# Norm outputs from factors in PSUM without GpSimd, and two output tiles side by side behind each head of a two-block network

## The chip, the cores and the metric

The kernel runs on one NeuronCore of a Trainium2 chip. The metric is the device time of one execution in microseconds (us); less is better. The core has TensorE (matrix products into PSUM), the vector engine (DVE), ScalarE (ACT), GpSimd (POOL), and SyncE (SP), which here only issues transfers.

## What is computed

Two transformer-like blocks, one after the other, on 512 tokens of width 1024. The first has a layer with attention and a long convolution, and a layer that pools over windows of tokens; each is followed by an MLP with squared ReLU. The second has two hybrid layers (a linear recurrence beside an attention with latents, then a gated feed-forward). All of them have the same form, of which this is the core:

```
y = x * rsqrt(mean(x * x) + eps) * g
a = y * (1 + scale) + shift
x = x + gate * (squared_relu(a @ w1) @ w2)
x = x + gate * ((silu(a @ w_gate) * (a @ w_up)) @ w_ffn_out)
proj = a @ w_in
pooled = mean over a window of tokens of a, minus a
```

## The kernel before

Tokens lie along the free dimension: x is eight tiles of 128 channels by 512 tokens. Every fp32 value enters a product as a pair: a high part rounded to 12 bits and a low part, the rest; three products (high with high, low with high, high with low; `mm3`, lines 458 to 460) make one of full accuracy. One output tile of 128 columns is 8 x 3 products of 128x512.

Weights come as portions of 512 KB through six buffers, in an order that `plan` writes down. A portion is loaded by SyncE (line 233), its high part is made by ScalarE (line 255), its low part by a subtraction (line 273). The engine of the subtraction is fixed by a table for some weights (GpSimd for the input weights `xl`, the gates and most of the attention's), and for all others, the MLPs' among them, it is `self.l_eng`. A buffer is loaded anew when the portion in it is done with. `prefetch(n)` emits this work for up to n portions ahead; `consume` takes the next portion and calls `prefetch(self.look)`. Between the weights stand portions of the modulation's matrices (`ada`), summed by GpSimd (lines 371 and 383). In the heads' weights the product with the shift is summed besides (`_shift_step`, line 309, on the vector engine).

All instructions are emitted in the order of the program text; each engine runs its own in that order and waits for the others by semaphores.

A *head* stands before each MLP, each hybrid layer and each gated feed-forward, six in all. `head` starts the first four output tiles of the next product from x times the gains, which needs no norm: 96 products in line 619. Meanwhile the sums of squares (line 574), the inverse roots (`rsqrt`, lines 548 to 556) and their broadcast into a PSUM tile (line 563) are made. ScalarE copies that tile to SBUF (line 636). Then `norm_mod` makes the norm's output for all tiles to come, for each of the eight blocks: a product with the factors (vector engine, line 658), the high part (ScalarE, line 663), the same in full fp32 (GpSimd, line 664), the low part (vector engine, line 682). After each second block a portion of weights is prepared, with GpSimd as `l_eng`. Behind that the head's four tiles are evacuated (line 643 and the caller's `evac`). The next output tiles follow through `gemm`, one after the other; `gemm` has a form `outer=n` that computes n tiles side by side, block by block of the contraction. There are six PSUM buffers for output tiles (`ps`) and two further ones (`pss`, for sums and broadcasts).

In the hybrid layers `conv(0)` to `conv(7)` are the first tiles behind the head, each with three vector operations from PSUM (line 1925); between them the sums of squares of the latents (line 574, from line 542) and their inverse roots and broadcast lie. In the pooling layer (`layer1`) products with the pool's weights come first, two halves (line 1786 evacuates them), then products with window tables, again two halves (line 1812 evacuates them into x, line 603 makes the next head's inputs).

Of the kernel before, what the change touches and what calls it, by code (L numbers as in the profile page):

```python
# [14 lines left out]
AF = mybir.ActivationFunctionType  # L15
# [39 lines left out]
class Weights:  # L55
    """h and l views of one part, by chunk of the contraction"""
# [9 lines left out]
# which engine takes which small operation, and the order of the steps that run beside each other  # L66
# [69 lines left out]
class Prog:  # L136
# [59 lines left out]
    def piece(self, label, src, parts):  # L196
        """src: dram view, rows x blocks x columns; parts: (kind, which blocks and columns of the view, extra), each loaded alone"""
        for kind, (k, n), extra in parts:
            p = dict(label=label, src=src[:, k, n], raw=None)
            self.pieces.append(p)  # L200
            self.parts.append((p, (kind, extra)))

    def wpiece(self, label, w, k0, kc, n0, nc_, by_k=False, shift=None):
        """shift: (layer, which) of the shift whose product with the weights is wanted besides"""
# [112 lines left out]
    def prefetch(self, n_ahead):  # L317
        """splits emitted up to n_ahead weight parts beyond the one consumed last"""
# [47 lines left out]
    def scaled(self, mode, out, x, sc):  # L366
        """out = x * sc, by the vector engine, by GpSimd or by the scalar engine"""
# [7 lines left out]
    def add_scaled(self, mode, out, x, sc):  # L375
        """out += x * sc, by the vector engine, by GpSimd or by the scalar engine and GpSimd"""
# [28 lines left out]
    def ada_tick(self, want=None):  # L405
        """the rest of sums that came ready a while ago, or of those wanted"""
# [14 lines left out]
    def flush_into(self, out, src):  # L421
        """A column of ada_r holds 32 entries, each as the sums over the four quarters of the partitions: add these up
        and put each entry on its partition."""
# [4 lines left out]
    def flush(self, layer):  # L428
        """the modulation vectors that are ready"""
# [32 lines left out]
    def gemm(self, label, x, n_tiles, evac, outer=0, looks=None):  # L462
        """x: list of (h, l) tiles, one for each 128 of the contraction; evac(m, psum)"""
# [38 lines left out]
    def steps(self, gen):  # L502
        """one step of the generator with each tick"""
# [91 lines left out]
    def head_x(self, k):  # L595
        """x times the norm's gains, ahead of the norm"""
# [8 lines left out]
    def head(self, chain, gs, sh, evac):  # L605
        """The first four tiles of a product with a norm's output start from x times the gains; the factor of each token
        and the product with the shift come on behind. chain() gives the factors. Returns the norm's output."""
# [25 lines left out]
        group(range(2, 3))  # L633
        bp = self.bcast(y, 4, self.ps_s, "pss")
        bc = self.get()
        self.S.copy(bc[:], bp[:])
        group(range(3, 8))
        l_eng, self.l_eng = self.l_eng, self.G
        A = self.norm_mod(self.x, bc, gs, sh, each=lambda k: self.prefetch(k // 2 + 1) if k % 2 else None)
        self.l_eng = l_eng  # L640
# [10 lines left out]
    def norm_mod(self, xs, bc, gs, sh, n=T, free=False, each=None):  # L651
        """h/l pairs of x * rstd * gs + sh"""
        out = []
        pend = None
        for k, x in enumerate(xs):
# [6 lines left out]
            else:  # L662
                self.S.activation(r(hl[0])[:, 0:n], t[:, 0:n], AF.Identity, scale=gs[:, k:k + 1], bias=sh[:, k:k + 1])
                self.G.tensor_scalar(y[:, 0:n], t[:, 0:n], gs[:, k:k + 1], sh[:, k:k + 1], op0=ALU.mult, op1=ALU.add)  # L664
# [20 lines left out]
    def gain(self, name, layer, i, g=None, width=8):  # L685
        """g * (1 + scale) as columns"""
# [9 lines left out]
    def sin_red(self, x, out, P, tmp, quarter=False):  # L696
        """out = sin(x), or cos(x); x is kept. In steps"""
# [84 lines left out]
    # parts split ahead by the last products before a norm: the head's parts are through before the last ones  # L782
# [73 lines left out]
    def hyena_filter(self, hd, w3):  # L856
        """Spectrum of the filter, in steps. With t and f both even or odd the transform falls into four of half the size:
# [893 lines left out]
    def layer1(self):  # L1751
# [40 lines left out]
        for half in range(2):  # L1792
# [23 lines left out]
            if half == 0:  # L1816
                self.prefetch(4)
# [583 lines left out]
```

## Time and profile before

| | us |
|---|---|
| median of three runs | 2698.91 (2698.41 to 2698.95) |
| span of the profiled execution | 2697.1 |
| TensorE busy | 2487.8 |
| vector engine busy | 1863.4 |
| GpSimd busy | 1567.3 |
| ScalarE busy | 1106.0 |

The span runs from the first to the last instruction of the one execution that was profiled; the time of a run has 1.8 us more than it by the median, which lie before and behind the instructions. Times within the profile are counted from the span's start. In the span, the first layer takes about 470 us, its MLP goes to about 860, the pooling layer to 895, the second MLP to 1254, the hybrid layers to 1972 and to the end. A row of the timeline gives start and duration in us, engine, line, operation, output and inputs, and in brackets the idle time of the engine before it and what ended that. Neighbours of one line are merged, with their count. DVE is the vector engine, ACT is ScalarE, POOL is GpSimd, PE is TensorE, SPq the queue of SyncE.

### The profile page before, as it was taken

How to read it: one execution, taken by the hardware profiler on the slowest of the kernel's cores; microseconds unless marked ns; L12 is line 12 of the kernel's file. 1: busy time of each engine (PE TensorE's matmuls, PEld its weight loads, DVE VectorE, ACT ScalarE, POOL GpSimd, SP SyncE). 2: the span in 40 equal slices, each digit the busy share in tenths (PEclk: the TensorE clock that was granted, in tenths of full speed). 3: DMA queues.
4: the chain of work that ended last, by engine and by line, in shares of the span. 5: the costliest groups of instructions: out<-in, count | busy, mean ns of one | idle time of the engine just before them, and what ended most of it. 6: DMA issues, size and time to landing. Idle time of an engine off the chain costs nothing.

```text
span 2697.1 us, 32008 instructions
## 1 busy us (share of the span) xinstructions
PE 2487.8 (92%) x11472; PEld 2068.4 (77%) x11472; DVE 1863.4 (69%) x2612; ACT 1106.0 (41%) x2057; POOL 1567.3 (58%) x1250
## 2 busy tenths in 40 slices
PE   7787778999989899999879999999999799999998
PEld 6665667787868688888668887888877688788887
DVE  6899988776666787766888667455477876733334
ACT  3446553433223433334466543222245654423231
POOL 6687756699981689963675348778146744400001
PEclk8788989999989899999889999999999899999999
DMA  7233332366673167662312235666422123233331
GB/s 244 83 118 102 109 94 86 95 191 199 200 218 97 51 177 210 213 177 72 96 57 67 87 92 164 182 192 201 117 75 81 49 81 117 71 102 94 95 91 50
DMA packets 433368, 330.30 MB, mean 122 GB/s; under 512 B 11799, under 2 KB 365207, under 8 KB 433208
## 3 DMA queue, kind: packets, MB, share of 16 engines
q1 hardware_dynamic: 429976, 322.22, 39.8%
q0 software_dynamic: 3232, 6.03, 0.7%
q8 instruction: 90, 1.47, 0.2%
q14 instruction: 70, 0.57, 0.1%
HBM read 319.82 MB, written 8.39 MB: 122 GB/s over the span
## 4 chain that ended last, share of the span: by engine, by line
PE 52%; DVE 8%; POOL 3%; ACT 2%; issue 2%; POOLq 0%; DVEq 0%; ACTq 0%
PE ps L458 16%; PE ps L460 16%; PE ps L459 16%; PE ps L477 2%; PE ps L619 1%; POOL slot L273 1%; DVE slot L1973 1%; POOL slot L664 1%; DVE slot L1925 1%; DVE slot L2038 1%; DVE slot L1961 1%; DVE slot L527 1%; PE ps L2029 0%; DVE slot L682 0%; PE pss L574 0%
## 5 line engine op out<-in xcount | busy, mean ns | idle before, releaser
L458 PE MATMUL ps<-slot 128*128 128x512 f32 (+2 forms) x3120 | 1209.2, 388 | 56.0 <-DVE slot L527 16.8
L460 PE MATMUL ps<-slot 128*128 128x512 f32 (+2 forms) x3120 | 1202.8, 386 | 45.8 <-DVE slot L682 24.7
L459 PE MATMUL ps<-slot 128*128 128x512 f32 (+2 forms) x3120 | 1200.8, 385 | 16.6 <-DVE slot L273 13.5
L458 PEld LDWEIGHTS ps<-slot 128*128 128x128 f32 x3120 | 603.4, 193 | 174.1 <-DVE slot L527 19.6
L460 PEld LDWEIGHTS ps<-slot 128*128 128x128 f32 x3120 | 602.4, 193 | 169.0 <-DVE slot L682 32.7
L459 PEld LDWEIGHTS ps<-slot 128*128 128x128 f32 x3120 | 602.9, 193 | 128.9 <-DVE slot L273 15.2
L255 ACT CAST slot<-raw 128x512 fp32r<-128x512 f32 (+1 forms) x764 | 425.8, 612 | 339.6 <-DMA raw<-in_mlp_w_dram 220.2
L383 POOL TENSOR_TENSOR slot<-slot 128x512 f32<-128x512 f32 x336 | 489.9, 1458 | 57.9 <-ACT slot L373 30.5
L273 DVE TENSOR_TENSOR slot<-raw,slot 128x512 fp32r<-128x512 f32 (+1 forms) x554 | 486.9, 922 | 36.7 <-ACT slot L255 32.0
L542 POOL TENSOR_TENSOR slot<-slot 128x512 f32<-128x512 f32 (+1 forms) x64 | 88.0, 1380 | 555.7 <-ACT slot L536 550.1
L273 POOL TENSOR_TENSOR slot<-raw,slot 128x512 fp32r<-128x512 f32 (+1 forms) x210 | 307.7, 1490 | 141.0 <-ACT slot L255 100.1
L371 POOL TENSOR_SCALAR slot<-raw,cols 128x512 f32<-128x512 f32 x192 | 206.1, 1076 | 58.0 <-DMA raw<-in_w_ada_dram 39.7
L371 POOL TENSOR_SCALAR slot<-raw,s_lat 128x512 f32<-128x512 f32 x144 | 154.9, 1079 | 6.4 <-DMA raw<-in_ada_w_dram 6.3
L619 PE MATMUL ps<-slot 128*128 128x512 f32 x576 | 145.5, 412 | 7.4 <-DVE slot L1812 7.4
L2187 DVE TENSOR_TENSOR slot<-slot,ps 128x512 f32<-128x512 f32 x40 | 27.5, 687 | 175.5 <-PE ps L460 175.5
L536 ACT ACTIVATE slot<-slot 128x512 f32<-128x512 f32 (+1 forms) x98 | 55.3, 575 | 214.4 <-DVE slot L1708 61.4
L619 PEld LDWEIGHTS ps<-slot 128*128 128x128 f32 x576 | 114.0, 200 | 32.5 <-DVE slot L1812 8.3
L526 ACT CAST slot<-slot 128x512 fp32r<-128x512 f32 x80 | 47.1, 619 | 190.0 <-DVE slot L2187 155.8
L664 POOL TENSOR_SCALAR slot<-slot,g,mod 128x512 f32<-128x512 f32 x48 | 57.2, 1198 | 85.8 <-DVE slot L658 85.8
L527 DVE TENSOR_TENSOR slot<-slot 128x512 fp32r<-128x512 f32 x75 | 81.7, 1110 | 35.7 <-ACT slot L526 35.7
L2212 DVE SCALAR_TENSOR_TENSOR slot<-ps,mod,slot 128x512 f32<-128x512 f32 x40 | 30.0, 749 | 102.2 <-PE ps L460 102.2
L416 DVE STREAM_TRANSPOSE slot<-slot 128x512 f32<-128x512 f32 x44 | 31.1, 706 | 94.7 <-POOL slot L383 94.6
(322 smaller groups left out, 2796.7 us busy)
## 6 DMA issues: line engine op xcount, KB each, us to landing
raw<-in_mlp_w_dram SPq DMA_DIRECT2D x128, 512.0 KB, 4.8
raw<-in_w_ada_dram SPq DMA_DIRECT2D x96, 512.0 KB, 4.4
raw<-in_ada_w_dram SPq DMA_DIRECT2D x88, 512.0 KB, 5.0
raw<-in_w_ffn_in_dram SPq DMA_DIRECT2D x88, 512.0 KB, 4.2
raw<-in_w_in_dram SPq DMA_DIRECT2D x56, 512.0 KB, 3.8
raw<-in_w_ffn_out_dram SPq DMA_DIRECT2D x32, 512.0 KB, 5.3
raw<-in_mix_w_dram SPq DMA_DIRECT2D x20, 512.0 KB, 3.9
raw<-in_w_out_dram SPq DMA_DIRECT2D x16, 512.0 KB, 4.1
```

Source lines behind the costliest of these rows:

```text
L255: self.S.copy(r(v), src[:, k:k + kk, :])
L273: eng.tensor_tensor(r(lv), src, v, op=ALU.subtract)
L371: self.G.tensor_scalar(out, x, sc, 0.0, op0=ALU.mult, op1=ALU.add)
L383: self.G.tensor_tensor(out, out, v, op=ALU.add)
L458: self.PE.matmul(out, lhsT=wh, rhs=xh, start=start, stop=False)
L459: self.PE.matmul(out, lhsT=wl, rhs=xh, start=False, stop=False)
L460: self.PE.matmul(out, lhsT=wh, rhs=xl, start=False, stop=stop)
L527: (eng or self.V).tensor_tensor(r(l)[:, 0:n], src, h[:, 0:n], op=ALU.subtract)
L536: self.S.activation(sq[:, 0:n], x, AF.Square, scale=scale)
L542: (eng or self.G).tensor_tensor(st["acc"][:, 0:n], st["acc"][:, 0:n], sq[:, 0:n], op=ALU.add)
L619: PE.matmul(ps[:], lhsT=w[i][:, m * 128:(m + 1) * 128], rhs=r(x[j])[:], start=(k == 0 and n == 0), stop=(k == 7 and n == 2))
L664: self.G.tensor_scalar(y[:, 0:n], t[:, 0:n], gs[:, k:k + 1], sh[:, k:k + 1], op0=ALU.mult, op1=ALU.add)
```

## The change

In the head, the norm's products read the factors where the broadcast left them, in PSUM; the copy to SBUF stays for the evacuations and is made behind the first block. The full fp32 form of each block (line 664) is made by ScalarE. Low parts of weights beside the norm go to the engine that `l_eng` has outside (the vector engine). The first portion is prepared ahead of the broadcast, the others behind the third, fifth and seventh block. Behind the heads, the first two tiles are computed side by side: in the MLPs, in the hybrid layers (`conv2`), and in the feed-forward. In the pooling layer, portions are prepared at other places, and from its second part on by the vector engine. The rest of the diff takes comments out; it is left out here.

```
 head:
         group(range(2, 3))
+        self.prefetch(1)
         bp = self.bcast(y, 4, self.ps_s, "pss")
+        group(range(3, 8))
         bc = self.get()
-        self.S.copy(bc[:], bp[:])
-        group(range(3, 8))
-        l_eng, self.l_eng = self.l_eng, self.G
-        A = self.norm_mod(self.x, bc, gs, sh, each=lambda k: self.prefetch(k // 2 + 1) if k % 2 else None)
-        self.l_eng = l_eng
+
+        def beside(k):
+            if k == 0:
+                self.S.copy(bc[:], bp[:])
+            elif k % 2 == 0:
+                self.prefetch(k // 2 + 1)
+
+        A = self.norm_mod(self.x, bp, gs, sh, each=beside)
 norm_mod:
-                self.G.tensor_scalar(y[:, 0:n], t[:, 0:n], gs[:, k:k + 1], sh[:, k:k + 1], op0=ALU.mult, op1=ALU.add)
+                self.S.activation(y[:, 0:n], t[:, 0:n], AF.Identity, scale=gs[:, k:k + 1], bias=sh[:, k:k + 1])
 mlp:
-        self.gemm("w1", A, 4, lambda m, ps: evac(h0, ps))
+        self.gemm("w1", A, 4, lambda m, ps: evac(h0, ps), outer=2)
 layer1, end of the first loop and second loop:
-            self.prefetch(half + 1)
+            self.prefetch(half + 2)
+        self.l_eng = V
 ...
                 self.head_x(m)
+                if m == 2:
+                    self.prefetch(4)
             self.put(Z, self.pb[2 * half:2 * half + 2])
-            if half == 0:
-                self.prefetch(4)
-        self.l_eng = V
 hybrid:
-        def conv(j):
-            ps = gemm1("xl")
+        def conv2(*js):
+            pss = []
+            self.tick()
+            self.ada_tick()
+            self.gemm("xl", A, 2, lambda m, ps: pss.append(ps), outer=2)
+            conv(js[0], pss[0])
+            self.tick()
+            conv(js[1], pss[1])
+
+        def conv(j, ps=None):
+            ps = ps or gemm1("xl")
 ...
-        conv(0)
-        conv(1)
+        conv2(0, 1)
 up:
-                self.gemm("fg", A, 2, lambda m, ps: evac_g(ps))
+                self.gemm("fg", A, 2, lambda m, ps: evac_g(ps), outer=2 if c == 0 and i == 1 else 0)
```

## Rows read from the trace of the kernel before

**Rows 1.** The page: busy time of TensorE and GpSimd, share, instructions.
```profile
PE 2487.8 (92%) x11472; PEld 2068.4 (77%) x11472; DVE 1863.4 (69%) x2612; ACT 1106.0 (41%) x2057; POOL 1567.3 (58%) x1250
```
**Rows 2.** Waits over the span: who for whom, us in total, times, longest.
```profile
PE ps L460 <- DVE slot L682: 24.7, 18, 2.2
```
**Rows 3.** Timeline of the head and norm at 1615 us.
```profile
1611.41 0.60 PE L563 MATMUL pss<-ident,ny 128*128 128x128 f32 x4
1611.77 13.88 PE L619 MATMUL ps<-slot 128*128 128x512 f32 x60
1612.10 0.59 ACT L636 COPY slot<-pss 128x512 f32<-128x512 f32 x1 [8.34 <-PE pss L563]
1612.72 0.69 DVE L658 TENSOR_TENSOR slot<-slot 128x512 f32<-128x512 f32 x1 [2.69 <-ACT slot L636]
...
1615.04 1.28 DVE L658 TENSOR_TENSOR slot<-slot 128x512 f32<-128x512 f32 x2
1615.76 0.81 ACT L663 ACTIVATE slot<-slot,mod,g 128x512 fp32r<-128x512 f32 x1 [1.43 <-DVE slot L658]
...
1616.48 1.13 ACT L255 CAST slot<-raw 128x512 fp32r<-128x512 f32 x2
1616.94 3.00 POOL L273 TENSOR_TENSOR slot<-raw,slot 128x512 fp32r<-128x512 f32 x2
1617.02 1.78 DVE L682 TENSOR_TENSOR slot<-slot 128x512 fp32r<-128x512 f32 x1 [0.69 <-POOL slot L664]
...
1625.48 0.39 PE L458 MATMUL ps<-slot 128*128 128x512 f32 x1
...
1633.74 0.50 PE L460 MATMUL ps<-slot 128*128 128x512 f32 x1 [2.15 <-DVE slot L682]
...
1634.20 1.75 DVE L682 TENSOR_TENSOR slot<-slot 128x512 fp32r<-128x512 f32 x1 [0.52 <-POOL slot L664]
...
1636.00 0.79 PE L460 MATMUL ps<-slot 128*128 128x512 f32 x1 [1.30 <-DVE slot L682]
```
**Rows 4.** Window of TensorE: length, busy (instructions), granted clock, DMA share, GB/s.
```profile
1636.60:1641.60 5.00, 5.00 (x13) 0.50 0.35 105
```
**Rows 5.** Windows of all engines: length, busy of PE, PEld, DVE, ACT, POOL, clock, DMA.
```profile
530.00:797.00 267.00, 253.46 (x1096) 208.21 (x1095) 183.55 (x192) 81.76 (x145) 257.44 (x210) 0.97 0.64 197
...
1645.00:1972.00 327.00, 327.00 (x1448) 270.91 (x1447) 182.48 (x232) 97.23 (x179) 210.75 (x179) 1.00 0.61 177
```
**Rows 6.** Timeline of GpSimd and of SyncE's queue behind the head at 490.
```profile
526.54 1.21 POOL L371 TENSOR_SCALAR slot<-raw,s_lat 128x512 f32<-128x512 f32 x1 [6.34 <-DMA raw<-in_ada_w_dram]
...
522.62 3.34 SPq L233 DMA_DIRECT2D raw<-in_ada_w_dram  x2
```
**Rows 7.** Timeline of the vector engine: a small norm's product, factors in PSUM.
```profile
1330.68 0.68 DVE L658 TENSOR_TENSOR slot<-slot,ps 128x512 f32<-128x512 f32 x1
```
**Rows 8.** Timeline behind the heads of the hybrid layers, vector engine and TensorE.
```profile
2008.16 2.47 DVE L643 TENSOR_TENSOR slot<-ps,slot 128x512 f32<-128x512 f32 x4
...
2015.92 0.69 DVE L542 TENSOR_TENSOR slot<-slot 128x512 f32<-128x512 f32 x1 [0.36 <-ACT slot L536]
2016.76 3.01 PE L574 MATMUL pss<-ones,slot 128*128 128x1 f32 x16 [2.50 <-DVE slot L542]
2017.11 4.54 DVE L1925 SCALAR_TENSOR_TENSOR slot<-ps,cols,slot 128x511 f32<-128x511 f32 x6 [0.49 <-ACT slot L1923]
...
2022.88 1.19 DVE L554 TENSOR_TENSOR na<-yi 128x4 f32<-128x4 f32 x1
...
1316.70 0.65 PE L563 MATMUL ps<-ident,ny 128*128 128x128 f32 x4 [3.75 <-DVE ny L556]
```
**Rows 9.** Timeline of the pooling layer, vector engine and TensorE.
```profile
882.12 6.78 DVE L309 SCALAR_TENSOR_TENSOR slot<-raw,mod,slot 128x512 f32<-128x512 f32 x4
...
889.61 0.80 PE L619 MATMUL ps<-slot 128*128 128x512 f32 x1 [6.53 <-DVE slot L1812]
```

## The prediction

> **What bounds the kernel now.** I read the page's busy shares first: TensorE is busy for 92% of the span, GpSimd for 58% [rows 1]. So time can be had only where TensorE waits or runs at the lower clock. The list of waits names such a place: it waited 24.7 us, 18 times, for the vector engine's subtraction in line 682, the low part of a norm's output [rows 2]. Cut by window, these are three waits in each of the six heads (about 490, 910, 1275, 1615, 1990 and 2330 us), 24.7 / 6 = 4.1 us a head.
>
> The timeline of one head shows why. The factors' broadcast ends at 1612.0, ScalarE copies it, and the first product starts at 1612.7 [rows 3]. TensorE's 60 head products take 13.88 us, so one takes 13.88 / 60 = 0.23 us, and at 1625.5 it starts the first tile that needs the norm's output. It needs one of the eight blocks every 3 x 0.23 = 0.7 us; the norm's last subtraction ends only at 1634.20 + 1.75 = 1635.95, which is 23.2 us after its start. So TensorE waits, the last times 2.15 and 1.30 us [rows 3]. A vector subtraction takes 0.6 us from start to start where it is undisturbed (two in 1.28 us), but 1.78 us beside a GpSimd subtraction that runs from 1616.94 [rows 3]: the two hold each other up, and both are in this norm's chain.
>
> The waits cost more than themselves. From 1636.6 to 1641.6, behind these waits, the granted clock was 0.50, the 1.2 GHz level [rows 4]. Its 12 products there take 0.43 us instead of 0.23: 12 x 0.2 = 2.4 us, with the two at the edges 2.9 us. The heads at 490, 910 and 2330 have the same pattern.
>
> **What a head is worth depends on what follows it.** From 1645 to 1972 TensorE is busy without a gap, 327.00 of 327 us [rows 5], and likewise from 940 to 1254 and from 2360 to 2660: what the heads at 910, 1615 and 2330 save stays saved. From 530 to 797 it is GpSimd that is full, 257.44 of 267 us, while TensorE has 253.46 [rows 5]: there the end is set by when GpSimd's work begins. Behind the two heads of the hybrid layers (1275, 1990) a chain on the vector engine goes on.
>
> **The change, head by head.** *No GpSimd in the norm.* The added parts are, for each of the eight blocks, one more ScalarE activation in place of the GpSimd operation, and for each of four weight portions two subtractions on the vector engine (in the hybrid heads most stay on GpSimd: the input weights have that engine fixed). The products read the factors in PSUM. The trace has the form: line 658 with one operand in PSUM takes 0.68 us [rows 7], against 0.69 from SBUF [rows 3], so I cost this at nothing and count the copy off the front: the first product starts at 1612.1. The Trainium skill (Perfetto Trace Analysis, Optimizing Scalar/DVE Operations) gives the vector engine about 125 ns of access overhead on PSUM and 60 on SBUF; by it each norm would be 8 x 0.065 = 0.5 us longer, and the sum below 1.5 us smaller, as three heads count it. The two rows above do not show it.
>
> *The new length.* ScalarE's activations start 0.72 us apart (1615.76 to 1616.48), a pair of casts takes 1.13 us [rows 3]. The first block goes through alone: product 0.69, two activations 1.54, subtraction, with hand-overs 3.1 us, and the vector engine's next product stands behind that subtraction. The copy of the factors for the evacuations now lies on ScalarE in that time (0.59 us, [rows 3]). The next product waits for it at most, if the two may not read one bank together, and it is through before the subtraction is. Then three rounds of two blocks and a portion: ScalarE 4 x 0.72 + 1.13 = 4.0 us, the vector engine 6 x 0.6 = 3.6 us, so 4.2 us with a hand-over; last block 3.1. Together 3.0 + 3 x 4.2 + 3.1 = 18.7 us, so the end is at 1630.8, against 1635.95: 5.1 us earlier. The bound on the other side: GpSimd, now free, can begin its modulation sums inside the norm and hold up the vector engine. One portion of these is loaded by then, three operations in the price of up to 1.1 us each (1.78 - 0.69): 1634.
>
> *Two tiles side by side.* TensorE now takes 6 products for each block, 1.37 us, and needs the last low part 46 products after its start: 1625.5 + 46 x 0.23 = 1636. Both ends above are before that. So the waits (4.1 us) and the low clock behind them (2.9 us) go: 7.0 us a head. PSUM covers it: the head holds four of six buffers, the pair takes the other two; the next tile, due at 1636.5, needs the first evacuation, 0.7 us behind the norm (1631.5 to 1634.7). Without that cover TensorE would wait for it up to 2 us a head.
>
> *Three heads before TensorE-bound stretches:* 3 x 7.0 = **21.0 us**. Bounds: 3 x 4.1 = 12 if the clock falls anyway, 23 if all goes.
>
> *The head at 490.* GpSimd starts its full stretch at 526.54, after waiting 6.34 us for a load, which SyncE could issue only at 522.62 [rows 6]. The load's buffer is freed by the vector engine's subtraction of the fifth weight portion, queued behind the four evacuations of the head, hence behind the norm. With a norm that ends 3 to 5 us earlier this load is issued as much earlier; I take **4.0 us**, bounds 0 and 7.0 (what TensorE saves). The 13.5 us that TensorE waits inside this stretch stay.
>
> *The two hybrid heads.* Behind the norm, the vector engine has four evacuations, the rotation and the sums of squares: from 2008.16 to 2015.92 + 0.69 [rows 8], 8.5 us. TensorE waited 2.50 us for them, and in the other hybrid layer 3.75 us, up to 1316.70, for the inverse roots behind [rows 8]. These waits are the chain's, so the chain's shift counts, not TensorE's. The pair of tiles does not help here: both evacuations now come behind it, but in the trace the vector engine's six operations for them stood together already, from 2017.11 [rows 8]. GpSimd keeps its subtractions there, so I take 4.5 of the 5.1 us: 2 x 4.5 = **9.0 us**. Bounds: 0, if the small operations of the inverse roots, up to 1.19 us each beside GpSimd [rows 8], are held up longer; 16, if they are no longer held up.
>
> *Pool layer.* Four multiplications of weights with the shift, 1.69 us each beside GpSimd, stop the vector engine for 6.78 us, and TensorE waits 6.53 us for the evacuation behind them [rows 9]. Now two of them come earlier and two after the third tile, with that portion's subtractions on the vector engine: 4 x 0.76 (undisturbed, 4.54 / 6 in line 1925, [rows 8]) to 4 x 1.69, and 2 x 0.6: 4.2 to 8 us in place of 6.78. The tile for which TensorE waits lies behind all of them. I take **0.5 us**, bounds -1.5 and 3.
>
> Sum: 21.0 + 4.0 + 9.0 + 0.5 = 34.5 us. The profiled execution has a span of 2697.1 us; the median of the runs is 2698.91, the 1.8 us lie around the span and stay. 2698.9 - 34.5 = **2664 us**.
>
> **The rivals.** *Only TensorE's stretches keep it:* the gains at 490 and in the hybrid layers are eaten by GpSimd and the vector chain. For: GpSimd is 96% full behind the first [rows 5]. Against: its start is tied to the norm's end. 2698.9 - 21 = 2678. *More goes:* the hybrid chains lose their second wait too, and the first head keeps 7.0: 28 + 16 + 3 = 47, 2652. *Slower:* the norm moves from two helpers to one. If GpSimd is busy through the whole norm, every vector operation with two SBUF operands costs 1.78 us: 14 x 1.7 + 8 x 0.6 = 28.6 us, the end at 1640.7, past the 1636 at which the pair needs it. From there on it decides: 4.7 us of waiting and the low clock as before, and what hangs on the norm's end is 5 us later in three heads: about 2714. For: 1.78 us is the row. Against: there is one loaded portion of work for GpSimd then. The Trainium skill (SBUF — State Buffer, Who interferes with whom) says that a vector operation with two SBUF inputs and a GpSimd operation that reads SBUF shut each other out for the whole of the one that came first, and that one with a single SBUF input is left alone; by it the 8 products from PSUM stay at 0.6, as they stand in this sum; 1.78 us beside GpSimd agrees [rows 3]. *It does not do what it says:* TensorE waits elsewhere at once, for PSUM or the third portion, within 5 us of 2699.
>
> **How the numbers follow.** The forecast has 0.64, with a range of its own from 2656 to 2674; only TensorE's stretches 0.16; more goes 0.12; slower 0.04; no effect 0.04. From 2650 to 2682 all but the last two and the edges is held, some 0.85. A measurement tells about 0.2% (5.4 us) from no change: faster 0.92, same 0.04, slower 0.04.
>
> **What would show it.** No wait of TensorE for the low part in the heads; granted clock 1.00 behind them; a norm of 17 to 21 us, without GpSimd in it; GpSimd's full stretch from about 522; the sums of squares in the hybrid layers 4 to 5 us sooner after the head. A norm over 24 us, or a new wait of TensorE for PSUM behind the pair, would make it wrong; an unchanged end of the stretch at 797 points to the first rival.

## The result and the profile after

The changed kernel takes 2661.56 us, the median of four runs (2654.41 to 2663.62), against 2698.66 us for the kernel before on the same chip: a ratio of 0.9857, 95% interval 0.9844 to 0.9870, so 37.1 us less. The forecast was 2664, with a range from 2650 to 2682. The profiled execution has a span of 2660.8 us, 36.3 less than that of before.

Where the time went, by the distance from one head to the next (from the first product of a head in line 619 to that of the next, in each profiled execution). The prediction calls the heads by the time of their waits, 490, 910, 1275, 1615, 1990 and 2330; in the kernel before their first products are at 473, 882, 1254, 1601, 1972 and 2312.

| stretch | before | after | difference | forecast |
|---|---|---|---|---|
| first layer, to the head at 473 | 473.1 | 474.5 | +1.4 | 0 |
| first MLP and pool layer | 409.4 | 404.4 | -5.0 | -4.0, -0.5 |
| second MLP, from the head at 882 | 371.8 | 362.9 | -8.9 | -7.0 |
| first hybrid layer | 346.2 | 341.9 | -4.3 | -4.5 |
| first feed-forward | 371.4 | 364.7 | -6.7 | -7.0 |
| second hybrid layer | 340.0 | 334.1 | -5.9 | -4.5 |
| second feed-forward to the end | 385.3 | 378.3 | -7.0 | -7.0 |

The fourteen profiled executions of this study, whose kernels all leave the first layer untouched, reach the head at 473 between 472.8 and 479.0 us. So the first row is no effect of the change, and a difference of 2 us in one stretch carries no argument by itself.

The page's busy shares after the change, to be read beside [rows 1]:

```profile
PE 2477.6 (93%) x11472; PEld 2066.3 (78%) x11472; DVE 1831.9 (69%) x2646; ACT 1136.4 (43%) x2105; POOL 1458.0 (55%) x1168
```

GpSimd lost 109 us of work, ScalarE took on 30, and the vector engine is busy 32 us less although it does 34 operations more: its operations got shorter. From the list of TensorE's waits after the change, two lines:

```profile
PE ps L459 <- DVE slot L273: 15.5, 5, 5.5
PE ps L563 <- DVE ny L556: 10.1, 4, 5.4
```

The wait for the norm's low part [rows 2] is not in the list any more. What is left of what the prediction spoke of: a wait for weights' low parts (line 273), 15.3 us of it in the first MLP; the inverse roots in the hybrid layers (7.9 of the 10.1 us); and 6.0 us in the pool layer, where the kernel before has 7.4.

The timeline of the head and norm that [rows 3] show at 1615, now at 1596 (start, duration, engine, line, operation, in brackets the idle time and what ended it):

```profile
1596.16 0.60 PE L563 MATMUL pss<-ident,ny 128*128 128x128 f32 x4
1596.52 7.75 PE L619 MATMUL ps<-slot 128*128 128x512 f32 x33
1596.80 0.69 DVE L663 TENSOR_TENSOR slot<-slot,pss 128x512 f32<-128x512 f32 x1 [2.38 <-PE pss L563]
1597.58 0.81 ACT L668 ACTIVATE slot<-slot,mod,g 128x512 fp32r<-128x512 f32 x1 [9.68 <-DVE slot L663]
1598.31 0.80 ACT L669 ACTIVATE slot<-slot,mod,g 128x512 f32<-128x512 f32 x1
1599.01 0.56 ACT L641 COPY slot<-pss 128x512 f32<-128x512 f32 x1
1599.14 0.69 DVE L687 TENSOR_TENSOR slot<-slot 128x512 fp32r<-128x512 f32 x1 [1.65 <-ACT slot L669]
1599.75 1.28 DVE L663 TENSOR_TENSOR slot<-slot,pss 128x512 f32<-128x512 f32 x2
...
1604.15 1.80 POOL L371 TENSOR_SCALAR slot<-raw,cols 128x512 f32<-128x512 f32 x2 [18.07 <-PE ps L619]
...
1605.31 0.68 DVE L663 TENSOR_TENSOR slot<-slot,pss 128x512 f32<-128x512 f32 x1
1606.04 1.29 POOL L383 TENSOR_TENSOR slot<-slot 128x512 f32<-128x512 f32 x1
1606.11 1.77 DVE L687 TENSOR_TENSOR slot<-slot 128x512 fp32r<-128x512 f32 x1
...
1610.23 4.02 PE L477 MATMUL ps<-slot 128*128 128x512 f32 x17
...
1615.80 0.69 DVE L687 TENSOR_TENSOR slot<-slot 128x512 fp32r<-128x512 f32 x1 [0.49 <-ACT slot L669]
```

The norm runs from 1596.80 to 1616.49, 19.7 us against 23.2. In the six heads it takes 20.0, 18.6, 17.5, 19.7, 17.5 and 18.2 us; 18.7 was forecast. From 1604 GpSimd is at its modulation sums, inside the norm, and one subtraction of the norm takes 1.77 us beside an addition of these (line 383, 1606.04): the bound that the prediction named, met in part. TensorE starts the pair at 1610.23, with no idle time ahead of it. Its window behind the head, where [rows 4] have 0.50, and the stretch of [rows 5] (length, busy of PE, PEld, DVE, ACT, POOL, granted clock, DMA share, GB/s; in the first of TensorE alone):

```profile
1612.00:1620.00 8.00, 8.00 (x37) 1.00 0.25 74
...
530.00:797.00 267.00, 251.70 (x1082) 206.13 (x1081) 179.09 (x192) 79.05 (x141) 257.21 (x212) 0.97 0.65 196
```

The first shows the clock at its full level behind the head; in the 8 us behind each of the other five norms it is 1.00 as well. The second is as before: GpSimd full, TensorE waiting 15.3 us inside. GpSimd's start there and the load ahead of it, to [rows 6]:

```profile
523.12 1.70 POOL L371 TENSOR_SCALAR slot<-raw,s_lat 128x512 f32<-128x512 f32 x1 [16.03 <-PE ps L460]
...
519.12 1.54 SPq L233 DMA_DIRECT2D raw<-in_ada_w_dram  x2
```

Both are 3.4 to 3.5 us earlier than before (about 522 was forecast); counted from the head's start, 4.8 to 4.9 us. The bracket of the first row names a product of TensorE; in the trace the load, for which this operation waits too, landed at the same time within 0.1 us.

### The profile page after: what moved, and what is told of

Its sections match the earlier page's. It is cut to its first block, busy times and chain, and to the rows that moved or that the text cites. A ratio compares the mean times of both kernels' runs of the same rounds, so it can differ in the third digit from the quotient of the medians.

```text
span 2660.8 us, 31920 instructions
## 1 busy us (share of the span) xinstructions
PE 2477.6 (93%) x11472; PEld 2066.3 (78%) x11472; DVE 1831.9 (69%) x2646; ACT 1136.4 (43%) x2105; POOL 1458.0 (55%) x1168
## 4 chain that ended last, share of the span: by engine, by line
PE 59%; DVE 19%; POOL 11%; ACT 4%; issue 3%; DMA 2%; SPq 0%; POOLq 0%; DVEq 0%; ACTq 0%
PE ps L458 17%; PE ps L459 16%; PE ps L460 16%; POOL slot L383 6%; POOL slot L371 5%; PE ps L619 4%; PE ps L477 3%; DVE slot L273 2%; DVE slot L1988 1%; DVE slot L527 1%; DVE slot L1940 1%; DVE slot L1550 1%; DVE slot L2053 1%; PE pss L574 1%; PE ps L1382 1%
## 5 line engine op out<-in xcount | busy, mean ns | idle before, releaser
L458 PE MATMUL ps<-slot 128*128 128x512 f32 (+1 forms) x3024 | 1168.7, 386 | 56.8 <-DVE slot L527 17.0
L460 PE MATMUL ps<-slot 128*128 128x512 f32 (+1 forms) x3024 | 1159.3, 383 | 20.8 <-DVE slot L527 9.2
L459 PE MATMUL ps<-slot 128*128 128x512 f32 (+1 forms) x3024 | 1161.0, 384 | 18.4 <-DVE slot L273 15.5
L458 PEld LDWEIGHTS ps<-slot 128*128 128x128 f32 x3024 | 583.4, 193 | 171.5 <-DVE slot L527 20.1
L460 PEld LDWEIGHTS ps<-slot 128*128 128x128 f32 x3024 | 582.3, 193 | 132.0 <-DVE slot L527 9.4
L459 PEld LDWEIGHTS ps<-slot 128*128 128x128 f32 x3024 | 583.4, 193 | 126.3 <-DVE slot L273 18.1
L273 DVE TENSOR_TENSOR slot<-raw,slot 128x512 fp32r<-128x512 f32 x588 | 510.2, 911 | 35.4 <-ACT slot L255 34.1
L273 POOL TENSOR_TENSOR slot<-raw,slot 128x512 fp32r<-128x512 f32 (+1 forms) x176 | 251.7, 1454 | 175.8 <-ACT slot L255 134.8
L619 PE MATMUL ps<-slot 128*128 128x512 f32 x576 | 147.5, 416 | 6.0 <-DVE slot L1818 6.0
L619 PEld LDWEIGHTS ps<-slot 128*128 128x128 f32 x576 | 115.0, 202 | 31.8 <-DVE slot L1818 7.4
L477 PE MATMUL ps<-slot 128*128 128x512 f32 x480 | 111.1, 390 | 4.1 <-ACT slot L526 2.8
L477 PEld LDWEIGHTS ps<-slot 128*128 128x128 f32 x480 | 89.7, 188 | 23.8 <-ACT slot L526 3.2
```

Source lines behind the costliest of these rows:

```text
L273: eng.tensor_tensor(r(lv), src, v, op=ALU.subtract)
L458: self.PE.matmul(out, lhsT=wh, rhs=xh, start=start, stop=False)
L459: self.PE.matmul(out, lhsT=wl, rhs=xh, start=False, stop=False)
L460: self.PE.matmul(out, lhsT=wh, rhs=xl, start=False, stop=stop)
L477: self.PE.matmul(ps[:], lhsT=w[k][i], rhs=xs[k][j], start=(k == 0 and n == 0), stop=(k == kc - 1 and n == 2))
L619: PE.matmul(ps[:], lhsT=w[i][:, m * 128:(m + 1) * 128], rhs=r(x[j])[:], start=(k == 0 and n == 0), stop=(k == 7 and n == 2))
```

## The experiments

Twelve kernels. Each ratio is to the kernel before, run on the same chip in the same session (medians of 2697 to 2701 us). "Norm" is the length of the norm in the heads of the second MLP and of the first feed-forward.

| kernel | median, us | ratio, 95% interval | norm, us |
|---|---|---|---|
| changed kernel | 2661.56 | 0.9857 [0.9844, 0.9870] | 18.6, 19.7 |
| pair alone | 2684.42 | 0.9941 [0.9928, 0.9954] | 23.2, 23.2 |
| no pair | 2663.40 | 0.9857 [0.9844, 0.9870] | 19.0, 19.7 |
| full form on GpSimd | 2658.10 | 0.9841 [0.9828, 0.9853] | 16.8, 17.0 |
| weights' low parts on GpSimd | 2658.65 | 0.9842 [0.9828, 0.9857] | 18.1, 18.1 |
| both on GpSimd | 2667.87 | 0.9891 [0.9875, 0.9908] | 20.1, 20.3 |
| factors from SBUF | 2671.64 | 0.9902 [0.9885, 0.9918] | 22.2, 22.2 |
| old pool layer | 2655.81 | 0.9842 [0.9827, 0.9857] | 18.6, 19.7 |
| half of the sums' products by ScalarE | 2659.01 | 0.9851 [0.9837, 0.9866] | 18.6, 19.7 |
| one chain of roots | 2655.83 | 0.9842 [0.9827, 0.9856] | 18.6, 19.7 |
| modulation spread | 2637.30 | 0.9784 [0.9767, 0.9801] | 18.6, 19.7 |
| spread, and two more | 2633.17 | 0.9766 [0.9751, 0.9780] | 16.8, 17.0 |
| before, spread alone | 2677.27 | 0.9924 [0.9911, 0.9938] | 23.2, 23.2 |

### The pair alone, and everything but the pair

The first takes the kernel before and adds the three uses of `outer=2` of the diff; the second takes them out of the changed kernel:

```
-        self.gemm("w1", A, 4, lambda m, ps: evac(h0, ps), outer=2)
+        self.gemm("w1", A, 4, lambda m, ps: evac(h0, ps))
...
-        conv2(0, 1)
+        conv(0)
+        conv(1)
...
-                self.gemm("fg", ..., outer=2 if c == 0 and i == 1 else 0)
+                self.gemm("fg", A, 2, lambda m, ps: evac_g(ps))
```

> The kernel before with the pair of tiles behind each head alone; norm, copy of the factors and pool layer as before. Theory A (two separate mechanisms: TensorE's waits in the three heads with nothing but products behind go by the pair or by the earlier end of the norm, whichever is there; the head at 490 and the hybrid layers gain by the earlier end alone): the norm still takes 23.2 us, its last low part (1635.95) just meets the pair's need (1636), so the 3 x 7.0 = 21 us of the heads at 910, 1615 and 2330 are gained and nothing in the other three: 2698.7 - 21 = 2678, between 2674 and 2684. Theory B (the pair is the main cause everywhere): 2662 to 2670. Theory C (the pair only moves the wait to its end): over 2688.

> The changed kernel without the pairs: the first tiles behind each head are computed one after the other again. A single tile needs the last low part 13.9 + 7 x 0.69 + 0.46 = 19.2 us after the norm's start; the norms of the changed kernel take 17.5 to 20.0 us. Theory A: at most 1 us of waiting in each head, so 2661.6 to 2666. Theory B: the waits of the heads come back, 3 x 7 = 21 us: 2680 or more.

Without the pairs nothing is lost: 0.9857, the same ratio as the changed kernel, and at most 0.6 us of waiting for the norm in a head (here the one at 1584, from the list of waits):

```profile
PE ps L460 <- DVE slot L687: 0.6, 2, 0.4
```

The pair alone gains 16 us of the 21 expected, just outside theory A's range, and the heads at 1609 and 2313 give what was forecast (-6.2 and -6.5 us in their stretches). (The stretches are those of its profiled execution, the longest of its six runs, 8.8 us over their median; it comes to the head at 889 6.7 us later than the kernel before.) In the two hybrid layers the pair only moves the wait, as the prediction had it: the waits for the norm go, and the wait for the sums of squares grows from 1.0 and 2.5 us to 6.7 and 7.3; with those for the inverse roots all these waits come to 10.0 and 7.9 us, against 9.6 and 7.9 before. The third head before products alone, at 889, gains nothing (+0.7 us). Its waits for the norm are gone too, but TensorE waits 40 us behind the norm's end. The chain there, in the kernel with the pair alone (SyncE's load of the positions, the vector engine's cast of them, its subtraction of weights, TensorE):

```profile
964.65 0.42 SPq L1828 DMA_DIRECT2D slot<-in_positions_dram  x1
...
968.60 1.39 DVE L1830 CAST slot<-slot 128x512 f32<-128x512 int32 x1 [5.51 <-DMA slot<-in_positions_dram]
...
975.62 1.28 DVE L273 TENSOR_TENSOR slot<-raw,slot 128x512 fp32r<-128x512 f32 x2
...
976.36 0.79 PE L459 MATMUL ps<-slot 128*128 128x512 f32 x1 [6.12 <-DVE slot L273]
```

and in the changed kernel:

```profile
946.42 0.42 SPq L1833 DMA_DIRECT2D slot<-in_positions_dram  x1
...
950.43 1.34 DVE L1835 CAST slot<-slot 128x512 f32<-128x512 int32 x1 [6.90 <-DMA slot<-in_positions_dram]
...
957.35 1.28 DVE L273 TENSOR_TENSOR slot<-raw,slot 128x512 fp32r<-128x512 f32 x2
...
958.09 0.50 PE L459 MATMUL ps<-slot 128*128 128x512 f32 x1 [0.18 <-DVE slot L273]
```

A load issued late behind the norm (it stands in SyncE's queue behind loads that wait for buffers) stops the vector engine, and the subtraction that TensorE needs is queued behind. Four kernels put numbers to it: the norm ends 46.8 us after the head's start with the pair alone, 44.8 with the factors from SBUF, 42.1 with both parts on GpSimd, 40.2 in the changed kernel, and TensorE waits there 6.12, 4.43, 2.79 and 0.18 us. So at 910 the norm's end is worth its own time, whether TensorE waits for the norm itself or not. What the pair does is real where it is alone and nothing where the norm is short.

### GpSimd's two parts in the norm, put back one by one

```
-                self.S.activation(y[:, 0:n], t[:, 0:n], AF.Identity, scale=gs[:, k:k + 1], bias=sh[:, k:k + 1])
+                self.G.tensor_scalar(y[:, 0:n], t[:, 0:n], gs[:, k:k + 1], sh[:, k:k + 1], op0=ALU.mult, op1=ALU.add)
```
is the first (full form); the second (low parts) is
```
+        l_eng, self.l_eng = self.l_eng, self.G
         A = self.norm_mod(self.x, bp, gs, sh, each=beside)
+        self.l_eng = l_eng
```
and the third has both.

> The changed kernel with the full fp32 form of each block on GpSimd again; the low parts of the weights stay on the vector engine. If GpSimd's subtractions of weights stretched the norm (theory P: two engines hold each other up at SBUF), most of the shorter norm stays, 19 to 20.5 us, and the time is 2661 to 2668. If the detour over GpSimd in each block's chain stretched it (theory H: hand-over to a slower engine), the norm is 22 us or more; the pair then still covers the heads at 910, 1615 and 2330, and the head at 490 and the hybrid layers lose their 13 us: 2672 to 2678.

> The changed kernel with the low parts of the weights beside the norm on GpSimd again; the full fp32 form stays on ScalarE. Theory P: the norm is 22 us or more, the head at 490 loses its gain (in the hybrid layers these subtractions are on GpSimd in either kernel): 2664 to 2672. Theory H: the norm stays at 17.5 to 20 us, shorter by up to 3 us without the vector engine's six subtractions: 2658 to 2663.

> The changed kernel with both the full fp32 form and the low parts of the weights beside the norm on GpSimd again: of the norm's change only the factors in PSUM are left. Each of the two alone on GpSimd kept the gain (norms of 16.5 to 19.5 us and 17.5 to 18.4 us). Theory F (the factors in PSUM shorten the norm, since a product takes 0.68 us instead of 1.2 beside GpSimd: 8 x 0.5 = 4 us): norm of 19 to 20.5 us, 2658 to 2668. Theory E (one of the two must leave GpSimd as well, or the chain through it is too long): norm of 22 us or more, and the time near that of the pair alone, 2674 to 2686.

Either part may stay on GpSimd: 0.9841 and 0.9842 are not to be told from the changed kernel. Theory H falls: with the full form on GpSimd the norm is the shortest of all, shorter than either theory had it, 16.5 to 17.2 us before MLPs and feed-forwards (in the hybrid layers, where GpSimd also subtracts, 18.9 and 19.5 instead of 17.5). Theory P falls with the low parts there, where it wanted 22 us and the norm takes 18.1. Each was a rule for one part; only both together are felt, with norms of 18.9 to 20.3 us and 8 to 9 us lost (by the medians' differences and by the ratios). That is theory F: what is left of the norm's edits then, the factors in PSUM and the new places of the portions, still keeps 3 of the 3.5 to 4.5 us. No run puts the places of the portions back alone, so the two are not told apart here. The mean of the norm's subtraction at the first feed-forward's head tells how the two parts add up: 0.75 us with the full form on GpSimd, 0.93 with the low parts, 1.33 with both. The changed kernel has 0.92 there, with GpSimd at its modulation sums; the kernel before has 1.24. Both on GpSimd, at the first feed-forward's head:

```profile
1611.42 3.06 DVE L689 TENSOR_TENSOR slot<-slot 128x512 fp32r<-128x512 f32 x1
1614.41 0.68 DVE L665 TENSOR_TENSOR slot<-slot,pss 128x512 f32<-128x512 f32 x1
...
1611.36 2.54 POOL L273 TENSOR_TENSOR slot<-raw,slot 128x512 fp32r<-128x512 f32 x2
```

The norm's subtractions (line 689 there) stretch beside GpSimd's, to 3.06 us at the worst, while the product from PSUM stays at 0.68. The full form alone on GpSimd:

```profile
1593.60 0.77 POOL L669 TENSOR_SCALAR slot<-slot,g,mod 128x512 f32<-128x512 f32 x1 [9.89 <-DVE slot L663]
...
1599.95 3.50 POOL L669 TENSOR_SCALAR slot<-slot,g,mod 128x512 f32<-128x512 f32 x2 [1.91 <-DVE slot L663]
...
1600.31 0.67 DVE L663 TENSOR_TENSOR slot<-slot,pss 128x512 f32<-128x512 f32 x1
1601.07 0.69 DVE L687 TENSOR_TENSOR slot<-slot 128x512 fp32r<-128x512 f32 x1
...
1601.02 0.82 ACT L668 ACTIVATE slot<-slot,mod,g 128x512 fp32r<-128x512 f32 x1 [0.38 <-DVE slot L663]
1601.74 1.13 ACT L255 CAST slot<-raw 128x512 fp32r<-128x512 f32 x2
```

Here GpSimd's record is as long (3.50 us for two), but the vector engine's operations stay at 0.7, and ScalarE, with one activation a block instead of two, waits for the vector engine. In the changed kernel ScalarE runs without a pause from the second block to the seventh in the norms that start at 901, 1258 and 2296, one round of two blocks and two casts in 3.9 to 4.1 us (at 1597 it waits twice more for the vector engine, 1.15 and 0.56 us): it has become the norm's bound, and outside the hybrid layers the move of the full form cost 2 to 3 us a norm which the time does not show.

### Factors from SBUF

```
+        self.S.copy(bc[:], bp[:])
...
-            if k == 0:
-                self.S.copy(bc[:], bp[:])
-            elif k % 2 == 0:
+            if k and k % 2 == 0:
                 self.prefetch(k // 2 + 1)
-        A = self.norm_mod(self.x, bp, gs, sh, each=beside)
+        A = self.norm_mod(self.x, bc, gs, sh, each=beside)
```

> The changed kernel with the norm's products reading the SBUF copy of the factors, made ahead of the norm as before. The copy takes 0.6 us ahead of the first product. If a product costs the same from either place (0.68 and 0.69 us in the trace of before) and GpSimd is idle beside most norms: three heads count it (490 and the two hybrid ones), 3 x 0.6 = 1.8 us more, 2662 to 2665. If the products from SBUF are held up by GpSimd (1.7 us instead of 0.7, several in a norm): the norms grow by 2 us and more, 2666 to 2672. If PSUM operands are slower: 2659 to 2661.

It loses 12 us, (0.9902 - 0.9857) x 2698.7; by the medians' differences 11, as expected for products held up by GpSimd. In the profiled executions 7.2 of 8.0 us lie in one stretch, that from the head at 882 on, where TensorE waits the 4.43 us given above and the granted clock falls to 0.60 for the 8 us from 963. The norm at 910 in this kernel, vector engine and GpSimd:

```profile
914.55 1.70 DVE L273 TENSOR_TENSOR slot<-raw,slot 128x512 fp32r<-128x512 f32 x2
916.18 1.78 DVE L663 TENSOR_TENSOR slot<-slot 128x512 f32<-128x512 f32 x1
...
912.29 3.42 POOL L371 TENSOR_SCALAR slot<-raw,cols 128x512 f32<-128x512 f32 x2 [18.37 <-PE ps L619]
915.80 1.61 POOL L383 TENSOR_TENSOR slot<-slot 128x512 f32<-128x512 f32 x1
```

and the same product in the changed kernel, while GpSimd is at the sums there too:

```profile
915.83 1.60 POOL L383 TENSOR_TENSOR slot<-slot 128x512 f32<-128x512 f32 x1
...
916.21 0.67 DVE L663 TENSOR_TENSOR slot<-slot,pss 128x512 f32<-128x512 f32 x1
```

The product is 1.78 us from SBUF and 0.67 with the factors in PSUM. The groups of these products over the whole span (busy us, mean ns of one, idle time ahead), changed kernel, factors from SBUF, kernel before:

```profile
L663 DVE TENSOR_TENSOR slot<-slot,pss 128x512 f32<-128x512 f32 x52 | 34.9, 680 | 13.5 <-PE pss L563 13.5
```
```profile
L663 DVE TENSOR_TENSOR slot<-slot 128x512 f32<-128x512 f32 x48 | 38.4, 811 | 14.8 <-ACT slot L639 14.8
```
```profile
L658 DVE TENSOR_TENSOR slot<-slot 128x512 f32<-128x512 f32 x48 | 55.8, 1173 | 22.3 <-ACT slot L636 22.3
```

680 ns from PSUM, 811 from SBUF with GpSimd at its sums only, 1173 with GpSimd in the norm too. The mean of six heads hides where it matters: at 910 it is 1009 ns from SBUF, and the products are 2.6 of the 3.6 us by which that norm is longer. At the first feed-forward's head they are only 0.5 of 2.5 us; the rest lies in subtractions that meet GpSimd's sums there. The Trainium skill (SBUF — State Buffer, Who interferes with whom) says that a vector operation with two SBUF inputs and a GpSimd operation that reads SBUF exclude each other, and that one with a single SBUF input does not take part unless it runs in a mode that uses both ports; these rows agree, 1.78 us against 0.67.

### The pool layer as before

```
-            self.prefetch(half + 2)
-        self.l_eng = V
+            self.prefetch(half + 1)
...
-                if m == 2:
-                    self.prefetch(4)
...
+            if half == 0:
+                self.prefetch(4)
+        self.l_eng = V
```

> The changed kernel with the pool layer as before (all portions prepared behind its first and second half, low parts on GpSimd). The prediction put the pool layer's part at 0.5 us with bounds -1.5 and 3: 2660 to 2664.6. A larger share of the gain, as the segment from the second head to the third shows 4.9 us less together with the first MLP: 2665 or more.

0.9842 against 0.9857, below both expectations: no gain by this part is seen, and if anything it costs a little; the intervals overlap.

### The stretch from 530 to 797

Two ways to take work off GpSimd there. In the first, ScalarE makes half of the products of the modulation's sums; in the second, the two last halves of a layer's modulation are computed one stretch later:

```
-        self.ada_mode = "G"
+        self.ada_mode = "GAA"
         self.mlp(0)
```
```
-        self.inter(self.mlp_plan(0), [(0, 10), (0, 11)] + [(1, h) for h in range(12)], lead=4, tail=6)
+        self.inter(self.mlp_plan(0), [(0, 10), (0, 11)] + [(1, h) for h in range(10)], lead=4, tail=6)
...
-        self.inter(seq, [(2, h) for h in range(12)], lead=5, tail=6)
+        self.inter(seq, [(1, 10), (1, 11)] + [(2, h) for h in range(10)], lead=5, tail=6)
...
-            self.inter(seq, [(3, h) for h in range(12)] if l == 0 else [], lead=8, tail=6)
+            self.inter(seq, [(2, 10), (2, 11)] + [(3, h) for h in range(12)] if l == 0 else [], lead=8, tail=6)
```

> The changed kernel; in the first MLP's stretch half of the modulation's multiplications (two portions of four) are made by ScalarE instead of GpSimd, the additions stay. Theory G (GpSimd sets the end of the stretch from 530 to 797; TensorE's three waits of 5.48, 5.53 and 3.91 us there are for it, by way of the vector engine's queue): these waits go, and with them the low clock behind them, some 2.4 us each: 14.9 + 7 = 22 us, 2636 to 2648. Rival (the stretch is set by the loads, or by TensorE): 2657 or more.

> The changed kernel with the last gate's portions of the modulation moved out of the first MLP's stretch (12 halves instead of 14) into the second MLP's, and of that one into the first feed-forward's (14 instead of 12). Theory G (the amount of GpSimd's work sets the stretch at 530 to 797, 257 us of 267; a seventh less is 37 us): half of TensorE's waits there or more go, with the low clock behind them, 8 to 20 us, and nothing comes back in the feed-forward (GpSimd 222 of 365 us there): 2640 to 2652. Rival (the waits come from the order of the queues: the vector engine stands at a sum or ScalarE at a load, whatever GpSimd's share; moving half of its products to ScalarE left the waits at 14 us): 2655 or more.

> The kernel before with only the modulation's portions spread as in the spread kernel. Theory G: TensorE's waits of 13.5 us inside the stretch from 530 to 797 go, with the low clock behind them; the head at 490 keeps its three waits of 4.4 us. The spread was worth 2661 - 2637 = 24 us to the changed kernel; if the changed head is worth the full 7.0 us at 490 once GpSimd is no longer full behind it, and only about 4 to 5 before, the spread is worth 20 to 23 us here: 2674 to 2678. If the head at 490 gained by GpSimd's earlier start alone, it is now worth 0 there: 2670 or less. If GpSimd's share is not what holds the stretch: 2690 or more.

The window of the stretch with ScalarE's help, and where ScalarE waits in it:

```profile
530.00:797.00 267.00, 252.82 (x1081) 205.60 (x1080) 171.29 (x190) 111.78 (x197) 196.57 (x159) 0.97 0.65 195
...
ACT slot L255 <- DMA raw<-in_mlp_w_dram: 102.4, 23, 9.9
```

and with the portions spread, in the changed kernel:

```profile
530.00:797.00 267.00, 267.00 (x1187) 221.29 (x1186) 186.99 (x204) 86.12 (x152) 228.75 (x185) 1.00 0.69 205
```

The first takes GpSimd from 257 to 197 us, and TensorE still waits 14.1 us. So GpSimd's busy share alone was not what held it; the products now stand in ScalarE's queue, between casts that wait 102 us in this stretch for loads of weights (129 in the changed kernel, where no sum stands behind them). The second takes fewer portions through the same buffers: GpSimd is at 229 us, TensorE never waits and has its full clock. The stretch from head to head is 404.4 - 381.3 = 23.1 us shorter, of which 15.3 are the waits and (1 - 0.97) x 267 = 8 the clock. Theory G, with GpSimd's time alone as the bound, falls by the first; that the amount of modulation put into the stretch sets it is shown by the second. Whether its loads or its operations do, stays open.

Spread alone on the kernel before is worth 21 us, on the changed kernel 20 (by the ratios) to 24 (by the medians), too near each other to tell what the head is worth. The stretches tell more. In the kernel before with the spread, the head keeps its three waits, 4.4 us together:

```profile
505.00:520.00 15.00, 10.62 (x39) 0.89 0.36 105
...
530.00:797.00 267.00, 267.00 (x1187) 221.34 (x1186) 188.15 (x207) 88.22 (x156) 236.71 (x189) 1.00 0.70 207
```

From head to head it is 385.8 us there against 381.3 with the change, so 4.5 us, not the 7.0 that TensorE should save where GpSimd does not hold it. Of the difference 0.07 x 26 = 1.8 us are the head itself, which ran at a granted clock of 0.93 in the profiled execution with the change and at 1.00 in that without.

### One chain of inverse roots, and the best kernel

In the hybrid layers the mean squares of both latents go into one tile of eight columns and one `rsqrt`:

```
-        yq = self.rsqrt(self.stat_ms(stq, 256, 1e-6), 4)
-        yk = self.rsqrt(self.stat_ms(stk, 128, 1e-6), 4)
...
+            V.tensor_scalar(ms2[:, 4 * i:4 * i + 4], ps[:, 0:4], 1.0 / width, 1e-6, op0=ALU.mult, op1=ALU.add)
+            self.put(s)
+        yqk = self.rsqrt(ms2, 8)
+        yq, yk = yqk[:, 0:4], yqk[:, 4:8]
```

> The changed kernel; in the hybrid layers the two inverse-root chains (queries and keys) are one chain on eight columns instead of two on four. TensorE waits there 5.39 and 1.02 us in the first hybrid layer and 1.49 us in the second. If the length of the chain sets these waits: the second wait of 1.0 us goes, and nothing but the sum of squares for the second factor comes ahead of the first: 2659 to 2662. If the small operations' waits for GpSimd set them (1.1 us instead of 0.16 in five of them) they stay as many: within 1.5 us of the changed kernel.

> As the kernel with the portions spread, and besides the full fp32 form on GpSimd in the four heads without hybrid layer (norms of 16.5 to 17.2 us there, against 18.2 to 20.0 with ScalarE) and one chain of inverse roots instead of two in the hybrid layers. If the shorter norm still pays where no wait is left in the head: 2 to 5 us under the spread kernel. If not: the same within 2 us.

The broadcasts of both factors, TensorE, with the single chain:

```profile
1298.16 1.97 PE L563 MATMUL ps<-ident,ny 128*128 128x128 f32 x8 [4.06 <-DVE ny L556]
...
1997.81 1.06 PE L563 MATMUL ps<-ident,ny 128*128 128x128 f32 x8
```

One wait of 4.06 us in place of 5.39 and 1.02, and none in place of 1.49: 3.8 us less waiting, and 0.9842 against 0.9857, more than expected, but with overlapping intervals. The last kernel has the spread, the single chain, and the full form on GpSimd in the four heads outside the hybrid layers: 2633.17 us, 0.9766 [0.9751, 0.9780], 63 us below the kernel before. It is the fastest of all, and 4 us below the spread alone, with intervals that overlap; which of its two additions gives that, and whether it is more than chance, is not shown.

## Why the prediction was right, and where it was not

The sum came to 34.5 us, and 37.1 were measured, term for term within 2 us of the table above. Of the marks that it set, these were met: no wait for the low part, the full clock behind the heads, a norm between 17 and 21 us, and no wait for PSUM behind the pair. The sums of squares in the second hybrid layer end 39.0 us after the head's start (1987.42) instead of 44.7: 5.7 us sooner, a little more than the 4 to 5 forecast:

```profile
1986.73 0.69 DVE L542 TENSOR_TENSOR slot<-slot 128x512 f32<-128x512 f32 x1 [0.36 <-ACT slot L536]
```

One mark was not met: GpSimd was to be out of the norm, and its modulation sums run inside it.

*TensorE-bound heads, 21.0 us.* 22.6 measured in the three stretches. The step "Two tiles side by side", from which the prediction concluded that the waits go, is right as arithmetic but gives the cause to the wrong part: it compared the norm's end only with the pair's need (1636 - 1612.7 = 23.3 us after the start) and never with that of a single tile. This needs the last low part seven blocks of 0.69 us and two products, 0.46 us, after its own start: by the prediction's numbers at 1625.5 + 5.3 = 1630.8, just where it put the norm's end. In the run without the pair that is 13.4 + 5.3 = 18.7 us after the norm's start; the norms of these three heads take 18.2 to 19.7 us, TensorE waits at most 0.6 us, and the time is the same. So the sum was right for the wrong part: the short norm alone is enough for it.

*"What the heads save stays saved."* Wrong for the head at 910. It was read from TensorE being busy without a gap from 940 to 1254, but such a stretch shows no gap also where the next queue is late by just the time that TensorE is. With the pair alone 6.12 us came back as a new wait at 976. The changed kernel escapes it by 0.18 us, because its norm ends early too.

*Factors in PSUM, "at nothing".* This step was mis-sized. The prediction compared 0.68 with 0.69 us, the two undisturbed rows [rows 3, 7], and left out that the product's mean in the norm of before was 1.2 us. Its own slower rival took 0.6 us for the products from PSUM and 1.78 for the others; the same numbers in the forecast would have shown a gain. The run without it loses 11 to 12 us, and with the factors in PSUM and the places of the portions left of the norm's edits, beside the pair and the pool layer, the ratio is 0.9891. That the norm still came out as long as forecast is in part luck: the sum had every vector operation at its undisturbed 0.6 us because GpSimd was to be gone. GpSimd came back into the norm, and at 910 it was the operand priced at nothing that kept the products short; from SBUF that norm takes 22.2 us.

*GpSimd out of the norm.* The forecast took both parts as one edit. They replace each other: one may stay. The length came out as forecast (18.7 against 17.5 to 20.0), with ScalarE at its bound as the sum had it. Two slips in that sum do not matter: it works out 3.1 us for the first block and adds 3.0, and the 0.6 us of a subtraction were read from two products (line 658). Counted from the pair alone (0.9941), the changes without the factors in PSUM are worth 10.5 us (0.9902), those without GpSimd's leaving 13.5 (0.9891), all together 22.7 (0.9857): of these two edits neither stands in for the other.

*Head at 490, 4.0 us.* Measured 5.0 with the pool layer, and GpSimd's start 3.4 us sooner. That the waits inside stay is shown (15.3 against 13.5). That GpSimd is what sets the end is only half right: less work for it, with as many portions, changed nothing.

*Hybrid heads, 9.0 us.* 10.2 measured: the chain's shift, as said. *Pool layer, 0.5 us.* Not seen in the time: with the old form the kernel is 4 to 5 us faster, with overlapping intervals, so whether the bound of -1.5 held stays open. TensorE's wait there is 6.0 us with the new form and 7.4 with the old. *Slower.* The rival needed GpSimd busy through the whole norm; it starts 7.3 us into it (1604.15 against 1596.80), and the products were left alone as that sum had it. Still, the rival's mechanism has its place: beside GpSimd, norms of up to 22.3 us from SBUF cost 11 to 12 us.

## What to carry over

Price an operand's place by the neighbour that runs beside it, not by the undisturbed row: the same product was 0.68 us from either place alone, and 0.67 against 1.78 beside GpSimd. Before two edits are added up, ask of each whether the other alone would do; here the pair, and one of GpSimd's two parts, were spare once the norm was short. And a stretch without a gap on the busiest engine does not prove that it has slack behind it: move that engine earlier in thought and look which queue is next, as the positions' load was here.

## What was not expected of the hardware

Small vector operations beside GpSimd pay as much as large ones, about 1 us. From the merged chain of inverse roots, eight columns wide, GpSimd's subtraction of weights and the vector engine:

```profile
1289.84 2.54 POOL L273 TENSOR_TENSOR slot<-raw,slot 128x512 fp32r<-128x512 f32 x2
...
1291.14 1.26 DVE L548 TENSOR_SCALAR yi<-ms 128x8 int32<-128x8 int32 x1
...
1294.40 1.19 DVE L554 TENSOR_TENSOR na<-ny 128x8 f32<-128x8 f32 x1
...
1297.54 0.17 DVE L554 TENSOR_TENSOR na<-ny 128x8 f32<-128x8 f32 x1
```

The same product is 1.19 or 0.17 us. The first guess of the root (line 548) has one input and is held up as well: it ends at 1292.40, GpSimd's two subtractions at 1292.38. The rule cited above covers that only by its exception, a mode that uses both ports; whether this operation ran in one, no row here shows. GpSimd's own operation of the full form took 0.77 us once and 3.50 for two beside the vector engine, whose products stayed at 0.67: there the delay fell on one side. The Trainium skill (Perfetto Trace Analysis, Optimizing Scalar/DVE Operations) gives the vector engine about 60 ns of access overhead on SBUF and 125 on PSUM, which would be, as an estimate, 65 ns more; here the product's record is 0.67 to 0.69 us from either.
